# HGRN2 level scores in pairs of levels and 32-column tiles, diagonal from score blocks, block copies on GpSimd

## The chip, the core and the metric

The kernel runs on one core of a Trainium2 chip. The metric is the device time of one execution in microseconds; the time before is the median of three runs. The five engines are called TensorE (PE, its weight loads PEld), VectorE (DVE), ScalarE (ACT), GpSimd (POOL) and SyncE (SP, which here only issues DMAs).

## What is computed

One inference step of a one-layer encoder with two parallel branches, mLSTM and HGRN2, for a prompt of 512 frames and a running stream of 32 frames. Both are projected by one large input matrix; the branches' outputs are merged by sigmoid gates, projected, and normalised. The part that matters here is the HGRN2 scan over 8 heads of 128 channels. In chunk form it is

```python
def _hgrn_chunk(S, inp):
    q, k, v, lf = inp
    causal = jnp.tril(jnp.ones((L, L), dtype=bool))[:, :, None]
    g = jnp.cumsum(lf, axis=2)
    dec = jnp.exp(jnp.where(causal, g[:, :, :, None, :] - g[:, :, None, :, :], -jnp.inf))
    a = jnp.einsum('bhtc,bhtsc,bhsc->bhts', q, dec, k)
    o = jnp.einsum('bhtc,bhce->bhte', q * jnp.exp(g), S) + jnp.einsum('bhts,bhse->bhte', a, v)
    ...
```

The score of query t and key s is a sum over channels c of q, k and a decay that depends on t, s and c. So it is no plain matrix product.

## The kernel before, in words

All sequences lie side by side in 544 columns: 32 of the stream (NS) and 512 of the prompt (NP). Activations have channels on the 128 partitions and time on the columns. The large products are done in split precision (three fp32r products for one fp32 product), and pairs of output tiles share a Strassen-like scheme of seven block products, the class `Two`; its `run` (L608) issues 12 matmuls of 128 stationary and 272 moving columns per block and gives way after the sixth. A `Pump` works through a list of such blocks; `pump.to(n)` advances it by half-blocks of six matmuls. TensorE's order is thus written by hand (manual_schedule), while the order on VectorE, ScalarE, GpSimd and the DMA queues is chosen by a scheduler that takes instructions under `high_priority` first.

**The HGRN stage** is `chain(h)` for each of the 8 heads. It is a generator: each `yield n` lets the pump run n half-blocks of the projections that the following heads need, then the chain's own matmuls are issued. Per head there are 28 half-blocks.

**Levels.** Time is halved recursively. At level c (1, 2, 4 to 64) a query in the odd block of length c meets the keys in the even block before it. The kernel keeps keys `kk` and queries `qq` in one tile and multiplies both in place by the decay products of each level (L1850), so that at level c a plain product gives the scores of pairs that are c apart. Because the first half of the prompt is stored reversed, `view` picks the columns by strides. Per level:

- ScalarE copies the keys in level order into `km` (L1818), and for the four levels below 16 the stream's keys and queries into `snap` (L1823);
- TensorE issues two products of 128 x 128, fp32, into the PSUM tile `pl` (L1832); at level 16 also the stream's own (L1834) and one for the four snapshots together (L1836);
- VectorE multiplies keys and queries (L1850), makes the decay products of the next level (L1853, L1856), and copies the scores that belong to this level under a mask into `at` (L1857, and L1861 for the stream).

The diagonal (t = s) is made apart: VectorE multiplies q and k for all 544 columns into `kq` (L1725), TensorE transposes this in five pieces (L1871), and VectorE sums each row into `dg` (L1873). After the last level GpSimd keeps the triangle of each score block (`triangle`, L1797, output `aa`). Then values and keys are transposed (L1902; L1903 for the stream, whose 32 columns GpSimd repeats four times, L1888), the state update follows (`su`, L1921, L1922), the states are chained on VectorE (L1927), and the output products are issued (`ho`, L1945 to L1949). The head before is finished in `finish`.

What TensorE waits for in this loop: the `km` copy, which waits for the update L1850, which waits for the products of the level before, since these read `qq` itself. The PSUM tiles `pl`, `pd`, `ht`, `su`, `ho` all come from one ring of two.

**A place with column tiles.** The stream's value products at the start (L1586) write to 32 partitions each (`vq[j * NS : (j + 1) * NS]`), so their stationary operand has 32 columns, and four such products stand on different column groups of the array. The dense value products around them are at L1576.

Of the kernel before, what the change touches and what calls it, by code (L numbers as in the profile page):

```python
# [17 lines left out]
P = 128  # L18
# [18 lines left out]
QUADS = P // NS  # L37
STEPS = (2, 3, 3, 3, 3, 3, 3)
# [29 lines left out]
def hybrid_step(ctx: ExitStack, tc: tile.TileContext, a, o):  # L68
# [247 lines left out]
    def masks():  # L316

        t = cp.tile([P, T], F32, tag="lm", name="lmask")
        u, n = t[:, :T].bitcast(U8), len(LEVELS) * HB
        return u[:, :n].rearrange("p (l t) -> p l t", l=len(LEVELS)), u[:, n : n + NS]  # L320
# [1060 lines left out]
    def level_masks():  # L1381
        lmask, smask = masks()
        sxt = small("sxt", [P, P + 2 * NS], bufs=1, tag="vsm")
        nc.sync.dma_start(sxt, a["sxt"])
        for i, c in enumerate(LEVELS):
            V.tensor_scalar(
                lmask[:, i, : 2 * P].rearrange("p (b t) -> p b t", b=2),
                sxt[:, :P].rearrange("p (o t) -> p o t", o=1).to_broadcast([P, 2, P]),
                float(c),
                None,  # L1390
                ALU.is_ge,
            )
        V.tensor_scalar(smask, sxt[:, P : P + NS], 0.5, None, ALU.is_ge)
        V.tensor_scalar(lmask[:, QUADS, 2 * P :], sxt[:, P + NS :], 0.5, None, ALU.is_ge)
        return lmask, smask
# [227 lines left out]
    with tc.manual_schedule(engines={mybir.EngineType.PE}):  # L1623
        for h in range(MH):
# [46 lines left out]
            if h == 0:  # L1671
                with tc.issue_after(last.ins):
                    next(bounds)
                    lmask, smask = level_masks()
# [21 lines left out]
    def units():  # L1696
# [19 lines left out]
        def query(h, qq):  # L1716
# [8 lines left out]
            V.tensor_tensor(kq[:, :T], q0[:, :T], kk[:, :T], ALU.mult)  # L1725
# [75 lines left out]
    def chain(h):  # L1801

        tf, kk, q0, qq, kq, ii = (hs[h][k] for k in ("tf", "kk", "q0", "qq", "kq", "ii"))
        at = tp.tile([P, NA + P], F32, tag="bc", name=f"at{h}")
        G.memset(at, 0.0)
        snap = small("snap", [P, 2, QUADS, NS], bufs=1, tag="ksm")
# [4 lines left out]
        tsmp = None  # L1811
        for li, c in enumerate(LEVELS):
            smp = li == QUADS
            n = HB if smp else NA
            km = tp.tile([P, NA], F32, tag="vs", name=f"km{h}{c}", bufs=1)
            pump.behind = held[-1] if held else None
            with tc.high_priority():
                low = S.copy(  # L1818
                    km.rearrange("p (n j c) -> p n j c", j=2, c=c),
                    view(kk, HB, ((2 * c, NA // (2 * c)), (c - HB, 2), (1, c))),  # L1820
                )
                if li < QUADS:
                    S.copy(snap[:, :, li], hs[h]["pair"][:, :, csmp])  # L1823
            held.append(low)
            yield STEPS[li]

            pn = paux(f"pl{h}{c}")
            for b in range(2):
                out, dims = pn[:, 0, b * P : (b + 1) * P], ((2 * c, P // (2 * c)), (HB + c, 2), (1, c))
                if c == 1:  # L1830
                    out, dims = out.rearrange("p (i s) -> p s i", s=2), (dims[1], dims[0])
                PE.matmul(out, km[:, b * P : (b + 1) * P], view(qq, b * P, dims), start=True, stop=True)  # L1832
            if smp:
                PE.matmul(pn[:, 0, NA:HB], kk[:, NA : NA + P], qq[:, csmp], start=True, stop=True)  # L1834
                ks, qs = (snap[:, i].rearrange("p l t -> p (l t)") for i in range(2))
                PE.matmul(pn[:, 1, :P], ks, qs, start=True, stop=True)  # L1836
# [4 lines left out]
            with tc.high_priority():  # L1841
# [15 lines left out]
                V.copy_predicated(at[:, :n], lmask[:, li, :n], pn[:, 0, :n])  # L1857
                if smp:
                    for i in range(QUADS):
                        d = slice(i * NS, (i + 1) * NS)  # L1860
                        V.copy_predicated(at[d, NA:HB], smask[d], pn[d, 1, d])  # L1861
# [4 lines left out]
            if li == 0:  # L1866

                yield 1
                pn = paux(f"pd{h}")
                for b, c_ in enumerate([c_ for c_, _, _ in chunks] + [slice(NA, NA + P)]):  # L1870
                    PE.transpose(pn[:, b // NB, b % NB * P : (b % NB + 1) * P], kq[:, c_], ident)  # L1871
                with tc.high_priority():
                    V.tensor_reduce(  # L1873
                        dg, pn.rearrange("p a t -> p (a t)")[:, : 5 * P].rearrange("p (b t) -> p b t", t=P), AX.X, ALU.add
                    )
# [11 lines left out]
        def quads(src, i):  # L1887
            G.tensor_copy(snap[:, i], src[:, csmp].rearrange("p (o t) -> p o t", o=1).to_broadcast([P, QUADS, NS]))  # L1888
            return snap[:, i].rearrange("p l t -> p (l t)")

        kt, it = kk[:, :NP], ii[:, :NP]
        ov = kq
        osb = small("osb", [P, P])
        kit = small("kit", [P, 2, P], tag="qw")
        kts, its = kit[:, 0], kit[:, 1]
        s0 = small("s0", [P, P], tag="qf")
        nc.sync.dma_start(s0, a["S0"][h])
        for n, src, dst, dss in ((0, ii, it, its), (2, kk, kt, kts)):
            yield n
            pt = paux(f"ht{h}")  # L1900
            for b, (c, _, _) in enumerate(chunks):
# [393 lines left out]
```

## Time and profile before

| | us |
|---|---|
| median of 3 runs (lowest, highest) | 1103.63 (1103.42, 1103.95) |
| profiled execution, first to last instruction | 1101.5 |
| HGRN stage in it | about 627 to 873 |

The page gives the profiled execution's span, and no other time of it. In the rows that follow, a group is named by line, engine, operation and tiles (output<-inputs); "PE L1832 MATMUL ... x4" in a timeline is four passes, since an fp32 product runs as two passes, each with its own weight load. The times of a matmul's end are modelled, so the starts, above all those of the weight loads, say more about how TensorE proceeds than the lengths.

### The profile page before, as it was taken

The page shows a single profiled execution, that of the slowest core. Times are in us where ns is not written, and L with a number is a line of the kernel's source. Part 1 is how long each engine was busy: PE and PEld are TensorE (multiplying, and loading weights), DVE is VectorE, ACT ScalarE, POOL GpSimd, SP SyncE. Part 2 cuts the span into 40 slices and gives each one's busy share as a digit, 9 for nine tenths or more (in the row PEclk, how much of TensorE's full clock was granted, in tenths as well). Part 3 has the DMA queues.
Part 4 walks back from the last instruction along what each step waited for, and adds up shares of the span by engine and source line. Part 5 has one row for each costly group of instructions (what it writes and reads, how often), then busy time and mean ns, then how long its engine had stood idle before and what let it go on. Part 6 is the DMA issues. An engine that isn't in the chain of part 4 may idle for free.

```text
span 1101.5 us, 23773 instructions
## 1 busy us (share of the span) xinstructions
PE 1092.4 (99%) x8625; PEld 1070.9 (97%) x8625; DVE 922.8 (84%) x2103; ACT 693.1 (63%) x1579; POOL 209.5 (19%) x375
## 2 busy tenths in 40 slices
PE   9999999999999999999999999999999999999997
PEld 9899999999999999999999999999999999999997
DVE  7889988686896786986888799999999977778885
ACT  7777557754666554665656476776776666446683
POOL 5204010303022021202120123232232210000002
PEclk9999999999999999999999999999999999999999
DMA  7135415639355276554798665666765683337753
GB/s 241 50 124 157 156 58 185 158 125 220 119 178 179 93 178 176 164 167 146 212 261 254 172 145 141 144 135 152 159 145 150 155 222 103 110 90 242 247 180 121
DMA packets 97262, 176.58 MB, mean 160 GB/s; under 512 B 11284, under 2 KB 18580, under 8 KB 96888
## 3 DMA queue, kind: packets, MB, share of 16 engines
q1 hardware_dynamic: 81072, 141.01, 39.9%
q0 software_dynamic: 15184, 32.93, 16.2%
q8 instruction: 68, 1.11, 0.4%
q10 hardware_dynamic: 888, 1.12, 0.3%
q14 instruction: 50, 0.41, 0.1%
HBM read 150.10 MB, written 41.69 MB: 174 GB/s over the span
## 4 chain that ended last, share of the span: by engine, by line
PE 93%; DMA 3%; DVE 2%; issue 1%; SPq 0%; ACT 0%; POOL 0%; ACTq 0%; POOLq 0%
PE d L608 44%; PE ya L167 9%; PE yb L167 4%; PE q L167 4%; PE k L167 4%; PE C L1077 4%; PE nm L1257 3%; PE sc L1037 2%; PE pl L1832 2%; PE u L291 2%; PE d L460 2%; PE vp L1576 2%; DMA ws<-in_w_in 1%; PE ple L167 1%; PE kt L1122 1%; PE ht L1902 1%
## 5 line engine op out<-in xcount | busy, mean ns | idle before, releaser
L495 POOL DMA_DIRECT2D ws<-in_w_in x46 | 40.2, 875 | 211.3 <-DVE hkq L1850 32.2
L622 ACT COPY t<-d 128x272 f32<-128x272 f32 x153 | 58.0, 379 | 14.0 <-PE d L608 14.0
L1850 DVE TENSOR_TENSOR hkq<-hkq,q 128x288 f32<-128x288 f32 (+1 forms) x96 | 40.7, 431 | 2.6 <-PE pl L1834 1.0
L785 DVE SCALAR_TENSOR_TENSOR cv<-ub,vec,cv 128x547 f32<-128x547 f32 x48 | 37.6, 784 | 1.6 <-ACT cv L780 1.2
L1832 PE MATMUL pl<-hkq,km 128*128 128x128 f32 x224 | 36.2, 283 | 0.6 <-ACT km L1818 0.5
L1818 ACT COPY km<-hkq 128x256 f32<-128x256 f32 x56 | 23.9, 428 | 14.2 <-DVE hkq L1850 5.2
L1832 PEld LDWEIGHTS pl<-hkq,km 128*128 128x128 f32 x224 | 30.3, 189 | 2.0 <-ACT km L1818 1.5
L1191 DVE SCALAR_TENSOR_TENSOR c<-c,wi,Cs 128x258 f32<-128x258 f32 x32 | 15.3, 479 | 18.8 <-PE Cs L1189 18.5
L1354 DVE TENSOR_TENSOR y<-ya,y 128x272 f32<-128x272 f32 x48 | 18.9, 435 | 12.1 <-PE ya L167 10.3
L1089 ACT COPY Co<-C 128x258 f32<-128x258 f32 x30 | 9.8, 378 | 27.3 <-PE C L1077 24.9
L1857 DVE COPY_PREDICATED at<-lmask,pl 128x256 f32<-128x256 uint8 (+1 forms) x56 | 25.2, 451 | 0.1
L777 POOL COPY uo<-ub 128x3 f32<-128x3 f32 x16 | 18.7, 1167 | 34.5 <-DVE ub L631 26.6
L1268 ACT COPY y<-nm 128x516 f32<-128x516 f32 x16 | 9.4, 590 | 23.0 <-PE nm L1257 22.5
L133 POOL TENSOR_TENSOR wple50l<-wple5r,wple50h 128x256 fp32r<-128x256 f32 x1 | 0.7, 736 | 120.9 <-ACT wple50h L132 120.9
L961 POOL COPY ksm<-kf 128x96 f32<-128x96 f32 x16 | 7.1, 445 | 84.9 <-ACT kf L975 84.9
L961 POOL COPY vsm<-vt 128x96 f32<-128x96 f32 x12 | 6.3, 525 | 85.9 <-ACT vt L633 43.5
L1797 POOL TENSOR_SCALAR_AFFINE_SELECT aa<-at 128x128 f32<-128x128 f32 x32 | 19.6, 643 | 8.2 <-DVE at L1857 8.0
L581 POOL DMA_DIRECT2D ws<-in_w_in x14 | 14.6, 1043 | 33.1 <-DVE ws272l L133 27.3
L1245 DVE BATCH_NORM_STATS2 bs<-y 128x6 f32<-128x512 f32 (+1 forms) x20 | 13.8, 692 | 8.3 <-ACT y L1268 8.0
L1257 PE MATMUL nm<-vhl,sh 128*128 128x258 f32 x112 | 18.4, 286 | 0.0
L376 POOL DMA_DIRECT2D w_pg_d<-in_w_pg x16 | 13.1, 818 | 25.1 <-issue 21.4
L1956 ACT ACTIVATE osq<-kq 128x128 f32<-128x128 f32 x32 | 9.8, 305 | 12.4 <-DVE kq L1951 12.1
(4735 smaller groups left out, 5086.7 us busy)
## 6 DMA issues: line engine op xcount, KB each, us to landing
ws<-in_w_in POOLq DMA_DIRECT2D x60, 256.0 KB, 4.9
ws<-in_w_in SPq DMA_DIRECT2D x46, 256.0 KB, 3.9
ya_d<-y SPq DMA_DIRECT2D x32, 272.0 KB, 2.3
y<-ya_d SPq DMA_DIRECT2D x24, 272.0 KB, 3.3
w_out_d<-in_w_out POOLq DMA_DIRECT2D x24, 256.0 KB, 6.5
w_pg_d<-in_w_pg POOLq DMA_DIRECT2D x24, 256.0 KB, 6.5
c<-in_C SPq DMA_DIRECT2D x16, 258.0 KB, 3.8
out_Cs<-c SPq DMA_DIRECT2D x16, 258.0 KB, 3.8
```

The source lines that it names most:

```text
L167: PE.matmul(both[b][:m, :TH], part(w, off + k * step, m, x), xx[:, half(b)], start=(k == 0 and j == 0), stop=(k == n - 1 and j == 2),)
L291: PE.matmul(both[b][:m, :TH], part(w, off + k * step, m, x), xx[:, half(b)], start=(k == 0 and j == 0), stop=(k == KD - 1 and j == 2),)
L495: G.dma_start(t, piece(u, i), accum_op=ALU.add)
L608: PE.matmul(ps, ww[:, c], xx, start=(start and k == 0 and j == 0), stop=end, skip_group_check=not start,)
L622: self.kept = S.copy(t, ps)
L785: V.scalar_tensor_tensor(cv[:, :547], ub[:, j : j + 547], vcol(V_CW + 4 * ft + j), cv[:, :547], ALU.mult, ALU.add)
L1077: PE.matmul(pn[g][:, :VH], kw[b][x][:, f * P : (f + 1) * P], vv[b][y][:, g * VH : (g + 1) * VH], start=(b == 0 and j == 0), stop=(b == NB ...
L1257: PE.matmul(pn[:, g, :VH], st[j][x][:, (i - j) * P : (i - j + 1) * P], vv[j][y][:, g * VH : (g + 1) * VH], start=(j == 0 and q == 0), stop ...
L1818: low = S.copy(km.rearrange("p (n j c) -> p n j c", j=2, c=c), view(kk, HB, ((2 * c, NA // (2 * c)), (c - HB, 2), (1, c))),)
L1832: PE.matmul(out, km[:, b * P : (b + 1) * P], view(qq, b * P, dims), start=True, stop=True)
L1850: V.tensor_tensor(x, x, d, ALU.mult)
L1857: V.copy_predicated(at[:, :n], lmask[:, li, :n], pn[:, 0, :n])
```

## The change

1. **Column tiles.** `scores` issues a level's products as pieces: for each of the two score blocks and each group of 32 keys one product with 32 stationary columns and max(c, 32) query columns, written to the 32 partitions of that group. The stream's keys and queries get such a product at each level below 32, once per group.
2. **Pairs of levels.** Level 1 is done with the diagonal, then 2 with 4, 8 with 16, 32 with 64. For the first of a pair the queries are copied too (`oldq`, and `olds` for the stream, in what is left of the mask tile), so that keys and queries can be multiplied on before TensorE reads them. The chain gives way once per pair, for the sum of both levels' steps.
3. **Diagonal.** Twenty products of 32 x 32 beside level 1 hold q times k; VectorE multiplies by an identity (`eye`) and sums five rows of 32. The product L1725 and the transposes L1871 go.
4. **Collecting.** Levels below 32 go under a mask into `near` (96 columns, five masks in place of seven). Level 32 is copied whole into `far` and level 64 straight into the off-diagonal halves of `at`, by ScalarE. At the end GpSimd copies the 32 x 32 blocks from `near` and `far` into `at`, and then makes the triangles as before. These copies are outside `high_priority`.
5. **Value transposes early.** `columns(ii, ...)`, the products with `dg` and the load of the state `s0` follow level 1; the keys' transposes stay behind the last level. The stream's columns are no longer repeated by GpSimd; a cleared tile `kit` takes the 32 rows.

```diff
+        def scores(pn, i, c, km, snap):
+            for b in range(2):
+                for g in range(QUADS):
+                    key, w = b * P + g * NS, max(c, NS)
+                    out = pn[g * NS : (g + 1) * NS, i, b * w : (b + 1) * w]
...
+                    PE.matmul(out, km[:, key : key + NS], ask, start=True, stop=True)
+            if c < NS:
+                for g in range(QUADS):
+                    PE.matmul(
+                        pn[g * NS : (g + 1) * NS, i, 2 * NS : 3 * NS],
+                        olds[:, 0] if snap else kk[:, csmp],
+                        olds[:, 1] if snap else qq[:, csmp],
...
+        def collect(ps, li, c):
+            if c < NS:
+                V.copy_predicated(near, lmask[:, li], ps[:, : 3 * NS])
+            elif c == NS:
+                S.copy(far, ps[:, : 2 * NS])
+            else:
+                for g in range(2):
+                    k = slice(g * c, (g + 1) * c)
+                    S.copy(
+                        at[k, :NA].rearrange("p (b s t) -> p b s t", b=2, s=2)[:, :, 1 - g],
...
         for li, c in enumerate(LEVELS):
-            km = tp.tile([P, NA], F32, tag="vs", name=f"km{h}{c}", bufs=1)
+            first_ = li % 2 == 1
+            if li % 2 == 1 or li == 0:
+                kms = tp.tile([P, 2, NA], F32, tag="vs", name=f"km{h}{c}", bufs=1)
+            km = kms[:, 0 if li % 2 else 1]
             with tc.high_priority():
+                if first_:
+                    S.copy(oldq..., view(qq, ...))
+                    if c < NS:
+                        S.copy(olds, hs[h]["pair"][:, :, csmp])
                 low = S.copy(km..., view(kk, ...))
-                if li < QUADS:
-                    S.copy(snap[:, :, li], hs[h]["pair"][:, :, csmp])
-            held.append(low)
-            yield STEPS[li]
+            if not first_:
+                held.append(low)
+                yield STEPS[li] + (STEPS[li - 1] if li else 0)
+                pn = paux(f"pl{h}{c}")
+                if li:
+                    scores(pn, 0, c // 2, kms[:, 0], True)
+                else:
...
+                            PE.matmul(
+                                pn[g * NS : (g + 1) * NS, 0, b * NS : (b + 1) * NS], kk[:, t_], q0[:, t_], start=True, stop=True
+                            )
+                scores(pn, 1, c, km, False)
...
-                V.copy_predicated(at[:, :n], lmask[:, li, :n], pn[:, 0, :n])
+            if not first_:
+                if li == 0:
+                    V.tensor_tensor(same, pn[:, 0, : (NB + 1) * NS].rearrange("p (b t) -> p b t", t=NS), eye, ALU.mult)
+                    V.tensor_reduce(dg, same, AX.X, ALU.add)
+                else:
+                    collect(pn[:, 0], li - 1, c // 2)
+                collect(pn[:, 1], li, c)
+            if c == 2 * NS:
+                for g in range(QUADS):
...
+                    G.tensor_copy(at[k, :NA].rearrange("p (b q s t) -> p b q s t", b=2, q=2, s=2)[:, :, g // 2], both_)
             if li == 0:
                 yield 1
-                    PE.transpose(pn[:, b // NB, b % NB * P : (b % NB + 1) * P], kq[:, c_], ident)
+                columns(ii, it, its)
```

How the instructions stand now, at three places. The names are the program's tiles with their numbers: `pl28` is the score tile of head 2 at level 8, `hkq2` holds its keys and queries, `lmask` the masks and the copied queries; rows of the changed kernel carry its own line numbers. On TensorE, head 2 before, from level 1 to level 16 (dense products left out):

```order
L1832 MATMUL pl21_9982<-hkq2_9364,km21_9959 128x2x64 x2
...
L1871 MATMUL pd2_10001<-ident_104,kq2_9365 128x128 x5
...
L1832 MATMUL pl22_10037<-hkq2_9364,km22_10008 128x128 x2
...
L1832 MATMUL pl24_10082<-hkq2_9364,km24_10044 128x128 x2
...
L1832 MATMUL pl28_10129<-hkq2_9364,km28_10089 128x128 x2
...
L1832 MATMUL pl216_10168<-hkq2_9364,km216_10136 128x128 x2
L1834 MATMUL pl216_10168<-hkq2_9364 128x32
L1836 MATMUL pl216_10168<-snap_9957 128x128
```

And now, to the last level:

```order
L1894 MATMUL pl21_10118<-q02_9852,hkq2_9430 32x32 x20
L1841 MATMUL pl21_10118<-hkq2_9430,km21_10096 32x2x16 x8
L1844 MATMUL pl21_10118<-hkq2_9430 32x32 x4
...
L1818 MATMUL ht2_10170<-ident_104,hi2_9703 128x128 x4
...
L1841 MATMUL pl24_10253<-lmask_2764,km22_10184 32x32 x8
L1844 MATMUL pl24_10253<-lmask_2764 32x32 x4
L1841 MATMUL pl24_10253<-hkq2_9430,km22_10184 32x32 x8
L1844 MATMUL pl24_10253<-hkq2_9430 32x32 x4
...
L1841 MATMUL pl264_10478<-lmask_2764,km232_10410 32x32 x8
L1841 MATMUL pl264_10478<-hkq2_9430,km232_10410 32x64 x8
```

Two products of 128 x 128 per level have become 8 to 12 of 32 columns, a visit holds two levels, and the values' transposes stand ahead of level 2. On ScalarE, head 2 before, levels 4 to 16:

```order
L1818 COPY km24_10044<-hkq2_9364 128x256
L1823 COPY snap_9957<-hkq2_9364 128x2x32
L132 CAST ws175h_10106<-ws175_9863 128x512
L622 COPY t16751_10065<-d510_9836 128x272
L1711 ACTIVATE hkq3_9838<-kq3_9839 128x256
L622 COPY t175_10098<-d750_10072 128x272
L1818 COPY km28_10089<-hkq2_9364 128x256
```

And now, levels 8 and 16:

```order
L1873 COPY lmask_2764<-hkq2_9430 128x256
L1878 COPY lmask_2764<-hkq2_9430 128x64
L1879 COPY km28_10283<-hkq2_9430 128x256
L1705 ACTIVATE tf3_10341<-kq3_9974 128x256
L634 ACTIVATE kq3_9974<-d510_9971 128x272
L1879 COPY km28_10283<-hkq2_9430 128x256
```

The first of a pair has three copies in a row (queries, stream, keys), and the second's copy of the keys follows after two instructions of the next head. On GpSimd, the end of head 2's scores before, and then now:

```order
L581 DMA ws175_9863<-in_w_in 128x512
L1888 COPY snap_9957<-hi2_9601 128x128
L495 DMA ws376_10340<-in_w_in 128x512
L1888 COPY snap_9957<-hkq2_9364 128x128
L1797 AFFINE_SELECT aa2_10283<-at2_9955 128x128 x4
L495 DMA ws153_10574<-in_w_in 128x512
```

```order
L582 DMA ws175_9997<-in_w_in 128x512
L496 DMA ws376_10543<-in_w_in 128x512
L1935 COPY at2_10089<-at2_10089 32x2x64 x4
L1790 AFFINE_SELECT aa2_10505<-at2_10089 128x128 x4
L582 DMA ws152_10299<-in_w_in 128x512
L496 DMA ws153_10842<-in_w_in 128x512
```

The four block copies stand directly ahead of the four triangles, and the weight DMAs of the next head stand behind both.

More of the change, by code (lines that the diff above doesn't have):

```diff
@@ L37 @@
 QUADS = P // NS
+SUB = 5
 STEPS = (2, 3, 3, 3, 3, 3, 3)
@@ L1803, in chain @@
         tf, kk, q0, qq, kq, ii = (hs[h][k] for k in ("tf", "kk", "q0", "qq", "kq", "ii"))
[L1804 to L1806 removed]
+        at = tp.tile([P, NA + 6 * NS], F32, tag="bc", name=f"at{h}")
+        near, far = at[:, NA : NA + 3 * NS], at[:, NA + 3 * NS : NA + 5 * NS]
+        G.memset(at[:, NA:], 0.0)
         dg = small("dg", [P, 5])
@@ L1811, in chain, with columns @@
         tsmp = None
+        kit = small("kit", [P, 2, P], tag="qw")
+        G.memset(kit, 0.0)
+        oldq, olds = old[:, :NA], old[:, NA : NA + 2 * NS].rearrange("p (l t) -> p l t", l=2)
+        eye = old[:, NA + 2 * NS :].rearrange("p (o t) -> p o t", o=1).to_broadcast([P, NB + 1, NS])
+        kt, it, ov = kk[:, :NP], ii[:, :NP], kq
+        kts, its = kit[:, 0], kit[:, 1]
+        osb = small("osb", [P, P])
+        s0 = small("s0", [P, P], tag="qf")
+        def columns(src, dst, dss):
+            pt = paux(f"ht{h}")
+            for b, (c, _, _) in enumerate(chunks):
+                PE.transpose(pt[:, 0, b * P : (b + 1) * P], src[:, c], ident)
+            PE.transpose(pt[:, 1, :P], src[:, NA : NA + P], ident)
+            with tc.high_priority():
+                S.copy(dst, pt[:, 0, :])
+                S.copy(dss[:NS], pt[:NS, 1, :P])
@@ L1868, in chain @@
                 yield 1
[L1869 to L1875, printed above, removed]
+                columns(ii, it, its)
+                nc.sync.dma_start(s0, a["S0"][h])
+                for b in range(NB):
+                    S.mul(ov[:, b * P : (b + 1) * P], it[:, b * P : (b + 1) * P], dg[:, b : b + 1])
+                S.mul(osb, its, dg[:, 4:5])
             if li == (4 if h < HH - 1 else 6) and h:
@@ L1884, in chain @@
                 triangle(aa[:, j, b], at[:, b * P : (b + 1) * P], 1 - 2 * j)
[L1887 to L1901, printed above, removed]
-                PE.transpose(pt[:, 0, b * P : (b + 1) * P], src[:, c], ident)
-            PE.transpose(pt[:, 1, :P], quads(src, n // 2), ident)
-            with tc.high_priority():
-                S.copy(dst, pt[:, 0, :])
-                if n:
-                    S.mul(dss, pt[:, 1, :P], 1.0 / QUADS)
-                else:
-                    S.copy(dss, pt[:, 1, :P])
-            if n == 0:
-                for b in range(NB):
-                    S.mul(ov[:, b * P : (b + 1) * P], it[:, b * P : (b + 1) * P], dg[:, b : b + 1])
-                S.mul(osb, its, dg[:, 4:5])
+        yield 2
+        columns(kk, kt, kts)
         yield 2
```

83 lines of the change are left out of this document (44 added, 39 removed).

## The prediction

> **What bounds the kernel now.** I read the page first: span, busy engines, and the chain that ended last.
>
> ```profile
> span 1101.5 us, 23773 instructions
> PE 1092.4 (99%) x8625; PEld 1070.9 (97%) x8625; DVE 922.8 (84%) x2103; ACT 693.1 (63%) x1579; POOL 209.5 (19%) x375
> PE 93%; DMA 3%; DVE 2%; issue 1%; SPq 0%; ACT 0%; POOL 0%; ACTq 0%; POOLq 0%
> ```
>
> TensorE is busy from end to end and holds 93% of the last chain. "Busy" alone proves little, because matmuls are pipelined, so I asked for the waits of TensorE over the whole span, and for the busy times of the HGRN stage, which is the only stage that the change touches.
>
> ```profile
> PE pl L1832 <- ACT km L1818: 0.5, 1, 0.5
> 627.00:873.00 246.00, 245.33 (x1993) 242.66 (x1992) 237.44 (x651) 175.00 (x485) 69.31 (x100) 1.00 0.64 148
> ```
>
> The first row is the only wait of TensorE inside the stage: 0.5 us in 246 us. In the second row the columns after the length are PE, PEld, DVE, ACT and POOL. TensorE issues without a break, so its time here is the sum of its passes. VectorE is at 237.4 of 246 us, but what it delivers is on time. A head takes about 30.7 us (246 us for eight heads), and a microsecond of TensorE time saved per head is worth 8 us at the end, as long as nothing starts to wait.
>
> **The change, TensorE's part.** What goes is read from the starts of the weight loads, which follow each other without gaps.
>
> ```profile
> 701.09 0.54 PEld L1832 LDWEIGHTS pl<-hkq,km 128*128 128x128 f32 x4
> 701.55 0.30 PEld L1834 LDWEIGHTS pl<-hkq 128*128 128x128 f32 x2
> 701.77 0.30 PEld L1836 LDWEIGHTS pl<-snap 128*128 128x128 f32 x2
> 701.99 0.19 PEld L608 LDWEIGHTS d<-xh,ws451h 128*128 128x128 f32 x1
> 690.05 0.58 PEld L1871 LDWEIGHTS pd<-ident,kq 128*128 128x128 f32 x5
> 690.60 0.19 PEld L608 LDWEIGHTS d<-xfh,ws251h 128*128 128x128 f32 x1
> ```
>
> An fp32 product is two passes. The two products of a level (x4) take 701.55 - 701.09 = 0.46 us, 115 ns a pass; the two sample products at level 16 take 0.22 us each; the five diagonal transposes 690.60 - 690.05 = 0.55 us. Per head: 7 x 0.46 + 0.44 + 0.55 = 4.21 us, over eight heads 33.7 us.
>
> What comes: per head 96 products with 32 stationary columns, 32 in the first visit (20 for the diagonal, 12 for level 1), then 24, 24 and 16. That is 192 passes in place of 37. They go to four column tiles in turn, 48 passes a tile; in 44 of these 32 columns move, in 4 (level 64) 64. Nothing in this stage works like that, but the start of the program has such a place. The timeline of the value products (L1576) around the sample value products (L1586, 32 stationary columns, four tiles):
>
> ```profile
> 46.79 0.40 PE L1576 MATMUL vp<-wv3h,x 128*128 128x512 f32 x1
> 47.03 0.40 PE L1576 MATMUL vp<-wv3l,x 128*128 128x512 f32 x1
> 47.36 0.62 PE L1586 MATMUL vq<-wv0r,xg 128*32 128x512 f32 x1
> 47.36 0.62 PE L1586 MATMUL vq<-wv1r,xg 128*32 128x512 f32 x1
> 47.81 0.59 PE L1586 MATMUL vq<-wv0r,xg 128*32 128x512 f32 x1
> 47.83 0.59 PE L1586 MATMUL vq<-wv3r,xg 128*32 128x512 f32 x1
> 48.35 0.72 PE L1576 MATMUL vp<-wv4h,x 128*128 128x512 f32 x2
> 48.91 0.40 PE L1576 MATMUL vp<-wv4l,x 128*128 128x512 f32 x1
> 47.35 0.11 PEld L1586 LDWEIGHTS vq<-wv0r,xg 128*32 128x32 f32 x1 [0.37 <-issue]
> 47.38 0.11 PEld L1586 LDWEIGHTS vq<-wv0r,xg 128*32 128x32 f32 x1
> ```
>
> Three things are to be seen. Different tiles run side by side: wv0r and wv1r both start at 47.36. One tile's second pass starts 47.81 - 47.36 = 0.45 us after its first, 0.88 ns a column, and its second load starts 0.03 us after its first load, while the first pass runs. And going in and out costs: dense passes stand 0.24 us apart, so the last ended at 47.27 and the tiles began at 47.36, 0.09 us; the last tile pass ended at 47.83 + 0.45 = 48.28, and the third dense pass at 48.91 puts the first at about 48.44, 0.16 us. I price a visit at 0.25 us, four visits at 1.0 us a head.
>
> The passes themselves: at 0.88 ns a column and with loads fully hidden, 44 x 28 + 4 x 56 ns = 1.46 us a head. With a tile's load (30 ns) and pass (28 ns) one after the other it is 44 x 58 + 4 x 86 = 2.9 us. I take 40 ns for the short pass and 70 for the long one, 2.04 us, nearer to the hidden end, since the rows show a load under a running pass. Then a head pays 1.0 + 2.04 = 3.04 us (2.46 to 3.9) for the 4.21 us removed: 1.17 us less, over eight heads 9.4 us (14 to 2.5).
>
> The value transposes (five passes) are only moved from behind the last level to behind the first; no pass is added, and the dense products between stay 28 half-blocks a head.
>
> **The other engines.** The groups of one head, 690 to 720 us, by form:
>
> ```profile
> L1857 DVE COPY_PREDICATED at<-lmask,pl 128x256 f32<-128x256 uint8 x6 | 2.7, 445 | 0.0
> L1861 DVE COPY_PREDICATED at<-lmask,pl 32x32 f32<-32x32 uint8 x4 | 0.8, 190 | 0.0
> L1873 DVE TENSOR_REDUCE dg<-pd 128x5 f32<-128x640 f32 x1 | 0.8, 819 | 0.0
> L1725 DVE TENSOR_TENSOR kq<-q,hkq 128x544 f32<-128x544 f32 x1 | 0.7, 720 | 0.0
> L1818 ACT COPY km<-hkq 128x256 f32<-128x256 f32 x7 | 3.0, 427 | 1.8 <-DVE hkq L1850 1.0 <-DVE hr L185 0.5 <-DVE rsq_u L184 0.4
> L1823 ACT COPY snap<-hkq 128x64 f32<-128x64 f32 x4 | 1.0, 247 | 0.0
> L1888 POOL COPY snap<-hi 128x128 f32<-128x128 f32 x1 | 0.6, 596 | 0.0
> L1888 POOL COPY snap<-hkq 128x128 f32<-128x128 f32 x1 | 0.3, 293 | 1.2 <-DVE hkq L1850 1.2
> 711.16 2.59 POOL L1797 TENSOR_SCALAR_AFFINE_SELECT aa<-at 128x128 f32<-128x128 f32 x4 [1.18 <-DVE at L1857]
> ```
>
> VectorE loses about 5 us of these (the level-16 mask copy with them) and gains five masked copies of 96 columns, about 0.26 us each on the line between 190 ns at 32 and 445 at 256 columns, and two operations over 160 columns, about 0.3 us each: some 3 us less in 30.7. That buys no time by itself, since TensorE did not wait for VectorE, but it loosens the tightest helper. ScalarE loses four snapshots (1.0 us) and gains three copies of the queries (427 ns each), two of the samples (247 each) and three block copies out of PSUM (about 250 each): about 1.5 us more, in an engine at 175 of 246 us. Neither counts on TensorE's path, except in the hand-over below. GpSimd loses the two broadcast copies and half a memset and gains a memset and four copies of 32 partitions; the mask tables are made once and under dense products.
>
> **The hand-over.** What is new is the wait. Before, TensorE did one level per visit, with 18 dense products until the next; now two levels in 36. The row of steps of one level before:
>
> ```profile
> 698.84 0.38 PE L608 MATMUL d<-xfh,wa2251h 128*128 128x272 f32 x1
> 699.21 0.46 DVE L1850 TENSOR_TENSOR hkq<-hkq,q 128x288 f32<-128x288 f32 x1
> 699.91 0.42 DVE L1850 TENSOR_TENSOR hkq<-hkq,q 128x256 f32<-128x256 f32 x1
> 700.44 0.41 ACT L1818 COPY km<-hkq 128x256 f32<-128x256 f32 x1 [0.48 <-DVE hr L185]
> ```
>
> From the resumption of dense work (698.84) to the end of the copy (700.85) is 2.0 us; the next level's load came at 701.09, so 18 products gave 2.25 us and 0.24 us were to spare. Now two such hops with three copies for the one (0.43 + 0.25 more), about 4.7 us, stand against 36 products, 4.5 us, plus the visit's own first half, 0.3 us or so, because only its second half needs the later copy. That is just enough. I put 0.2 us of waiting per head into the sum, 1.6 us.
>
> Sum: -9.4 + 1.6 = -7.8 us. The profiled span of 1101.5 becomes 1093.7; the runs of before have a median of 1103.6, 2.1 us above the span, which is outside the first and last instruction and stays: 1095.8 us.
>
> **The rivals.**
>
> *Passes do not overlap (chance 0.12).* The four tiles of the rows above had passes of 512 columns, sixteen times longer than these; no row shows short ones. If short passes start one by one at the 30 ns of a load whatever their tile, 192 take 5.8 us, with the visits 6.8, and a head is 2.6 us longer: 21 us, 1124 us. Against it stands that loads of different tiles began within 10 ns. The Trainium skill (TensorE: Matmul & The Clock Gate, section "Wait — 56ns, not 53.3ns?") puts the start-to-start of matmuls at no less than about 25 ns however few columns move; an estimate by that page is 192 x 25 ns = 4.8 us, 1116 us. The rows at 47.36 speak against it, as far as they go.
>
> *The hand-over decides (chance 0.15, slower).* The wait that the copies make takes the place of the time saved. If on each of the two VectorE hops one more 0.7 us instruction stands ahead, half of it covered, visits two to four wait 0.7 us each: 24 x 0.7 = 17 us, against 9.4 saved: 1111 us. It decides from 0.39 us a visit. For it: the slack was 0.24 us, and VectorE issues in order. Against: VectorE has 3 us less to do per head, and masked copies no longer stand ahead of the updates.
>
> *It does not do what it says (chance 0.09).* Loads and passes of a tile serialize and something is lost at each start; the price comes to the 4.2 us removed: 1103.6, within 0.2%.
>
> *GpSimd is late (chance 0.07).* After the last level come ScalarE's copies (about 1.5 us), four GpSimd copies (0.3 to 0.6 us each by the rows of L1888), and the four triangles, 2.6 us: 5.3 to 6.5 us. TensorE reaches the output products after 36 dense products (4.5 us), five transposes (0.55) and ten state passes at 0.11 us (1.1): 6.15 us. It loses at most 0.35 us a head, 3 us: 1098.6, still faster.
>
> **How the numbers follow.** My forecast has 0.57. Its own range is 1088 (cheapest passes, no wait, a little from the loosened VectorE) to 1103 (dearest passes). A measurement of this kernel tells 0.2%, 2.2 us, from no change. Faster by more than that: 0.53 of the forecast and the late GpSimd, 0.60. Within: 0.04 of the forecast and the third rival, 0.13. Slower: 0.15 + 0.12 = 0.27. The range takes in the hand-over and leaves the first rival out: 1088 to 1111 us.
>
> **What would show it.** In the profile after, the weight loads of a visit of 64 passes should span about 0.6 to 0.9 us until the dense products go on, the next ones less; four tiles should start within some 30 ns of each other. If loads stand 25 ns or more apart throughout, the first rival holds. Waits of TensorE for the query or key copies should stay under 2 us in all; 10 or more is the second. VectorE should fall by about 25 us in the stage. The forecast is wrong if the stage is not shorter, or if the saving appears in the stage and is lost behind it.

## The result, and the profile after

The changed kernel takes 1091.93 us (median of 4 runs, 1091.56 to 1093.22) where the kernel before takes 1103.72 (1103.42 to 1103.95): a ratio of 0.9892, 95% interval 0.9879 to 0.9904, 11.8 us less. The forecast was 1095.8, 7.9 us less; the range of 1088 to 1111 holds the time. The profiled execution is the longest of the four.

The page after, span, engines and the chain that ended last:

```profile
span 1091.5 us, 26220 instructions
PE 1082.2 (99%) x9865; PEld 1055.3 (97%) x9865; DVE 896.1 (82%) x2052; ACT 700.6 (64%) x1611; POOL 220.1 (20%) x399
PE 89%; DVE 4%; DMA 4%; issue 1%; ACT 1%; POOL 0%; ACTq 0%; DVEq 0%; SPq 0%; POOLq 0%
```

TensorE still bounds the kernel. The HGRN stage, from its first score product to its last output product, in the busy times by stretch (before, then after; columns as in the prediction):

```profile
627.75:870.62 242.87, 242.20 (x1968) 239.53 (x1966) 235.21 (x646) 173.52 (x479) 67.84 (x99) 1.00 0.64 147
```

```profile
628.06:861.46 233.40, 231.40 (x3206) 223.80 (x3206) 211.45 (x607) 181.18 (x512) 78.14 (x121) 1.00 0.66 154
```

The stage is 9.5 us shorter in these two executions. VectorE has 23.8 us less to do in it, ScalarE 7.7 more, GpSimd 10.3 more. The waits of TensorE in the stage after:

```profile
PE ht L1818 <- DVE hkq L1911: 1.4, 2, 0.8
PE d L609 <- DVE ws288l L134: 0.6, 1, 0.6
```

No wait for a copy of queries or keys is among them. The profiled execution is the slowest of its four; in that of c_after below (the changed kernel once more) the first row is 0.3 us in place of 1.4.

**A visit.** The timeline of TensorE around the second visit of head 2 (48 passes), dense products ahead and behind:

```profile
693.59 0.29 PE L609 MATMUL d<-xh,wa1175l 128*128 128x272 f32 x1
693.81 0.33 PE L1841 MATMUL pl<-lmask,km 128*32 128x32 f32 x16
693.96 0.25 PE L1844 MATMUL pl<-lmask 128*32 128x32 f32 x8
694.02 0.32 PE L1841 MATMUL pl<-hkq,km 128*32 128x32 f32 x14
...
694.37 0.39 PE L609 MATMUL d<-xh,wa1175h 128*128 128x272 f32 x1
694.60 0.29 PE L609 MATMUL d<-xl,wa1175h 128*128 128x272 f32 x1
```

The start of the first product behind a visit can't be taken as it stands (the next comes 0.23 us after it, where dense ones stand about 0.125 apart), so I measure from the last dense product ahead (693.59) to the second behind (694.60): 1.01 us, less two dense slots, 0.76 us for the visit. In the same way one level of head 2 before:

```profile
698.31 0.29 PE L608 MATMUL d<-xh,wa1275l 128*128 128x272 f32 x1
698.44 0.66 PE L1832 MATMUL pl<-hkq,km 128*128 128x128 f32 x4
698.84 0.38 PE L608 MATMUL d<-xfh,wa2251h 128*128 128x272 f32 x1
699.06 0.29 PE L608 MATMUL d<-xfl,wa2251h 128*128 128x272 f32 x1
```

That is 0.75 - 0.25 = 0.50 us. Measured like this over all heads (from the third dense product ahead to the fourth behind, less six slots of 0.1237 us), the medians are: before, a level 0.489, level 16 with the stream 0.907, the five diagonal transposes 0.559, level 64 0.571 (it stands with the values' transposes: 1.127 for both, less 0.556 for these); after, the visits 0.916 (64 passes), 0.772 (48, twice) and 0.697 (32). Sixteen passes more or less are 0.144 us, 9 ns a pass, 36 ns a pass of one tile; what is left of each visit, 0.34 us, is the price of going in and out. The rows show the same: the 16 passes of the first kind start at 693.81, the next kind at 693.96. The slot is a little short: the dense products of the stage stand 0.126 us apart in the median, and with that every stretch is some 0.012 us shorter. The price per pass does not move by it; the price of going in and out becomes 0.33 us, and what is summed over the heads below differs by 0.3 us between before and after.

**The hand-over.** Between the second and the third visit of head 2, copies of the keys (L1879) and the third visit's loads; the rows between them left out:

```profile
698.32 0.42 DVE L1911 TENSOR_TENSOR hkq<-hkq,q 128x256 f32<-128x256 f32 x1
...
698.77 0.41 ACT L1879 COPY km<-hkq 128x256 f32<-128x256 f32 x1
...
699.11 0.22 PEld L1841 LDWEIGHTS pl<-lmask,km 128*32 128x32 f32 x16
...
699.29 0.25 PEld L1841 LDWEIGHTS pl<-hkq,km 128*32 128x32 f32 x15
```

The second copy ends at 699.18, while the visit's first half runs, 0.11 us ahead of the load that reads it. The other two hops have about 1 us more, since the values' transposes or the finish of the head before, with a half-block each, lie in them; the finish is missing from this place in the first and the last head, and there the third hop is as tight as the second. GpSimd at the end of a head, by groups of the page:

```profile
L1935 POOL COPY at<-at 32x128 f32<-32x128 f32 x32 | 21.7, 678 | 8.4 <-DVE wa1282l L134 6.7
L1790 POOL TENSOR_SCALAR_AFFINE_SELECT aa<-at 128x128 f32<-128x128 f32 x32 | 16.1, 536 | 0.6
```

Block copies and triangles take 4.7 us a head, and no wait of TensorE for them is among the rows. The mean of the block copies hides a spread: 0.28 us at the least, 0.51 in the median, and four of the 32 take 2.0 to 2.1 us, for a reason that stays open.

### The profile page after: what moved, and what is told of

Same layout as the page of the kernel before. It is cut to its first block, busy times and chain, and to the rows that moved or that the text cites. A ratio compares the mean times of both kernels' runs of the same rounds, so it can differ in the third digit from the quotient of the medians.

```text
span 1091.5 us, 26220 instructions
## 1 busy us (share of the span) xinstructions
PE 1082.2 (99%) x9865; PEld 1055.3 (97%) x9865; DVE 896.1 (82%) x2052; ACT 700.6 (64%) x1611; POOL 220.1 (20%) x399
## 4 chain that ended last, share of the span: by engine, by line
PE 89%; DVE 4%; DMA 4%; issue 1%; ACT 1%; POOL 0%; ACTq 0%; DVEq 0%; SPq 0%; POOLq 0%
PE d L609 41%; PE ya L168 9%; PE yb L168 4%; PE q L168 4%; PE k L168 4%; PE C L1078 4%; PE sc L1038 2%; PE u L292 2%; PE d L461 2%; PE vp L1570 2%; PE nm L1258 2%; DMA ws<-in_w_in 2%; PE ple L168 1%; PE pl L1841 1%; DMA kv_d<-vhl 1%
## 5 line engine op out<-in xcount | busy, mean ns | idle before, releaser
L1879 ACT COPY km<-hkq 128x256 f32<-128x256 f32 x56 | 23.7, 424 | 0.0
L1935 POOL COPY at<-at 32x128 f32<-32x128 f32 x32 | 21.7, 678 | 8.4 <-DVE wa1282l L134 6.7
L2001 ACT ACTIVATE osq<-kq 128x128 f32<-128x128 f32 x32 | 9.8, 305 | 13.4 <-DVE kq L1996 13.1
L377 POOL DMA_DIRECT2D w_pg_d<-in_w_pg x16 | 13.1, 818 | 24.4 <-issue 20.2
L377 POOL DMA_DIRECT2D w_out_d<-in_w_out x16 | 13.5, 1004 | 14.3 <-issue 12.5
L1790 POOL TENSOR_SCALAR_AFFINE_SELECT aa<-at 128x128 f32<-128x128 f32 x32 | 16.1, 536 | 0.6
L1258 PEld LDWEIGHTS nm<-vhl,sh 128*128 128x128 f32 x112 | 15.4, 190 | 0.5 <-ACT Co L1090 0.3
```

Of the source, the lines that this page charges most:

```text
L377: G.dma_start(late[g][n][k], src, accum_op=ALU.add)
L1258: PE.matmul(pn[:, g, :VH], st[j][x][:, (i - j) * P : (i - j + 1) * P], vv[j][y][:, g * VH : (g + 1) * VH], start=(j == 0 and q == 0), stop ...
L1879: low = S.copy(km.rearrange("p (n j c) -> p n j c", j=2, c=c), view(kk, HB, ((2 * c, NA // (2 * c)), (c - HB, 2), (1, c))),)
```

## The experiments

My theory after the result: TensorE's own sum decides (passes of 9 ns, 0.34 us to enter and leave), and the waits stay where they were because every hop fits, the tightest by 0.1 us. The rivals: the narrow passes alone are the gain; or VectorE's relief is; or one of the smaller moves (values, block copies, urgency) is.

The last column is the time that all the chain's own matmuls take on TensorE in the stage, measured as above around each stretch of them and summed over the eight heads. Waits are in it, their own and those of the dense products right beside them. In the first pair it is 77.3 us before and 66.7 after.

| kernel | median us | before, timed beside it | ratio (95%) | chain on TensorE, us |
|---|---|---|---|---|
| c_after, the change again | 1092.08 | 1104.48 | 0.9887 (0.9872, 0.9902) | 65.4 |
| e1_tiles_single | 1100.24 | 1104.72 | 0.9960 (0.9946, 0.9974) | 73.6 |
| e2_stream_once | 1094.69 | 1104.72 | 0.9911 (0.9896, 0.9925) | 67.3 |
| e3_diag_old | 1102.16 | 1104.72 | 0.9973 (0.9961, 0.9986) | 76.9 |
| e4_short | 1099.70 | 1104.72 | 0.9957 (0.9942, 0.9972) | 75.1 |
| e5_shift | 1105.08 | 1104.48 | 1.0006 (0.9997, 1.0015) | 77.4 |
| e6_copies_act | 1095.92 | 1104.48 | 0.9924 (0.9911, 0.9938) | 69.8 |
| e7_values_late | 1098.94 | 1104.48 | 0.9952 (0.9936, 0.9969) | 71.4 |
| e8_urgent | 1097.22 | 1104.23 | 0.9946 (0.9929, 0.9963) | 69.9 |
| e9_load | 1093.96 | 1104.23 | 0.9904 (0.9889, 0.9918) | 67.3 |
| e10_shift_add | 1093.44 | 1104.23 | 0.9903 (0.9888, 0.9918) | 67.2 |
| e11_add | 1092.66 | 1104.23 | 0.9896 (0.9881, 0.9911) | 66.4 |

A thousandth of the ratio is 1.1 us. Against c_after's ratio, the kernels' last column and their time rise together: what these edits do, they do on this chain. "Over the change" below means by the difference of the two ratios. Only e5 to e7 were timed beside c_after; with the ratio of the first pair, 0.9892, each of these figures is 0.6 us smaller.

**c_after.** 

> The changed kernel itself, unaltered, timed beside the next three on their chip. Expected 10 to 12 us under the kernel before, as in its first runs.

It came out so, 12.4 us under the kernel before.

**e1_tiles_single: tiles without pairs.**

```diff
-            first_ = li % 2 == 1
+            first_ = False
...
-                yield STEPS[li] + (STEPS[li - 1] if li else 0)
+                yield STEPS[li]
...
-                if li:
-                    scores(pn, 0, c // 2, kms[:, 0], True)
```

> The changed kernel with its column tiles and its diagonal, but one level per visit: seven visits a head instead of four, no copies of the queries. Theory (entering and leaving a visit is what costs: 0.34 us, and a pass 9 ns, by the gaps in the dense products around the visits of 64, 48 and 32 passes): three more visits are 3 x 0.34 x 8 = 8 us more than the changed kernel, so about 1100 us, only 3 to 4 us under the kernel before. Rival (the narrow passes are the gain, and the pairing only a convenience): within 2 us of the changed kernel, 1090 to 1094. Second rival (the pairing costs waits that single levels do not have): under 1091.

It is 8.1 us over the change, and 4.5 under the kernel before: the theory's number. The visits of 24 passes cost 0.536 us (median of 32), which again is 0.32 + 24 x 9 ns. So a level with the stream in narrow passes, 0.54, costs more than the 0.49 of its four wide passes. Alone, the tiles pay at level 16, where the stream's wide products go (0.907 before), and at level 1, where the diagonal rides along; the rest comes when two levels share one way in and out. The rival of narrow passes alone is refuted. Pairs in wide passes were not run; as four wide passes, which start 0.119 us apart, pay only 0.01 us beyond their own time (0.489 less four of 0.119), an estimate from these prices is that three visits fewer would save 3 x 0.01 x 8 = 0.2 us.

**e2_stream_once: fewer passes, unevenly.**

```diff
             if c < NS:
-                for g in range(QUADS):
+                for g in range(1):
...
-                V.copy_predicated(near, lmask[:, li], ps[:, : 3 * NS])
+                V.copy_predicated(near[:, : 2 * NS], lmask[:, li, : 2 * NS], ps[:, : 2 * NS])
+                V.copy_predicated(near[:NS, 2 * NS :], lmask[:NS, li, 2 * NS :], ps[:NS, 2 * NS : 3 * NS])
```

> The changed kernel with the stream's product of each level below 32 issued for the first group of 32 partitions only (the other three are multiplied by zero later), and its masked copy as a piece of its own of 32 partitions (five more short VectorE instructions a head). 30 of 192 passes a head go, all from three of the four column tiles; the first tile keeps its 48. If a visit lasts as long as the queue of passes (8 to 9 ns each, whatever the tile): 30 x 0.0085 x 8 = 2 us less than the changed kernel, about 1090. If it lasts as long as the fullest tile (32 to 36 ns a pass of one tile): no change, 1091 to 1093. If the five VectorE instructions delay the hand-over: above 1094.

The visits did get shorter, 0.855 and 0.702 us for 0.916 and 0.772: six passes gone take 0.06 us off the first visit and twelve 0.07 off the next two, 10 and 6 ns each, nearer to the queue's case than to the fullest tile's. The time did not: 2.6 us over the change, where the two intervals still overlap. What is lost is not the hand-over, as I had expected of the third case, but at the dense products, which wait for the splits of their weights:

```profile
PE d L609 <- DVE ws288l L134: 1.3, 1, 1.3
PE d L609 <- DVE ws276l L134: 0.3, 1, 0.3
...
PE d L609 <- DVE ws279l L134: 0.3, 1, 0.3
```

With the new instructions the scheduler's order on VectorE is another: ahead of the split of `ws274` stand a masked copy and an operation on a dense result that stand behind it in c_after. In six heads the stretch beside it, the transposes of `finish`, takes 1.16 us instead of 0.56.

**e3_diag_old: the diagonal of before.** The product L1725, the transposes and the sum come back, and the twenty products of 32 x 32 go (short form):

```diff
+            V.tensor_tensor(kq[:, :T], q0[:, :T], kk[:, :T], ALU.mult)
...
-                    V.tensor_tensor(same, pn[:, 0, : (NB + 1) * NS].rearrange("p (b t) -> p b t", t=NS), eye, ALU.mult)
-                    V.tensor_reduce(dg, same, AX.X, ALU.add)
...
+                pn = paux(f"pd{h}")
+                for b, c_ in enumerate([c_ for c_, _, _ in chunks] + [slice(NA, NA + P)]):
+                    PE.transpose(pn[:, b // NB, b % NB * P : (b % NB + 1) * P], kq[:, c_], ident)
...
                 columns(ii, it, its)
```

> The changed kernel with the diagonal of before: the product of queries and keys over 544 columns on VectorE, five transposes of 128 x 128 on TensorE, one sum over 640 columns; the first visit has 24 passes instead of 64. TensorE by the prices: five transposes 0.56 us for 40 passes of 9 ns, 0.2 us a head more, so 1.6 us in all, about 1093.5. Rival (the 0.9 us a head that VectorE gets back are what loosens the hand-over): waits of TensorE come back with it, 1096 or more.

9.5 us over the change: the rival, not the sum. The waits of TensorE, and the third visit of head 2 in the timeline:

```profile
PE pl L1842 <- ACT km L1880: 2.4, 6, 0.5
PE ht L1819 <- DVE hkq L1905: 2.3, 4, 0.9
```

```profile
699.62 0.42 DVE L1905 TENSOR_TENSOR hkq<-hkq,q 128x256 f32<-128x256 f32 x1
...
699.92 0.33 PE L1842 MATMUL pl<-lmask,km 128*32 128x32 f32 x16
...
700.26 0.40 ACT L1880 COPY km<-hkq 128x256 f32<-128x256 f32 x1
...
700.72 0.33 PE L1842 MATMUL pl<-hkq,km 128*32 128x32 f32 x16 [0.40 <-ACT km L1880]
```

Here the update stands 0.3 us ahead of the visit (after: 698.32 against 699.11, 0.8 us), so the visit breaks in two. The hand-over is the change's weak place, and the new diagonal is part of what holds it. Measured by stretches and summed over the heads, the third visits take 3.5 us more than their median after the change, the keys' transposes, which wait for the last update, 5.9 (4.2 of it in two heads), the state's products 2.0, and the passes themselves 1.3. This execution is the slowest of ten that lie between 1099.4 and 1104.5 us, so the shares are rough.

**e4_short: a shorter hand-over.**

```diff
-                yield STEPS[li] + (STEPS[li - 1] if li else 0)
+                yield STEPS[li] + (STEPS[li - 1] - 1 if li else 0)
```

> The changed kernel with five half-blocks ahead of each pair instead of six (30 dense products instead of 36; the rest run later). It asks how much slack the hand-over has. If it is just enough, as the record has it and as the copy that ends 0.1 us ahead of its use shows: visits two to four each wait about 0.6 us, 24 x 0.6 = 14 us, 1104 to 1108. If VectorE and ScalarE get the steps earlier because what was ahead of them in their queues is later too: half of that or less, 1092 to 1098.

7.7 us over the change, between the two cases: visits two to four are 0.74 us earlier each, 17.8 us in all, and less than half of that comes back as waits.

```profile
PE pl L1841 <- ACT km L1879: 6.5, 10, 1.1
PE ho L1990 <- POOL aa L1790: 2.0, 2, 1.5
```

So the hop from the second visit to the third gives way at once, those with 1 us to spare mostly do not. The second row is new: where TensorE arrives earlier, it meets GpSimd's triangles.

**e5_shift and e10_shift_add: one half-block elsewhere.**

```diff
-                yield STEPS[li] + (STEPS[li - 1] if li else 0)
+                yield STEPS[li] + (STEPS[li - 1] - (li == 2) if li else 0)
...
-        yield 2
+        yield 3
         columns(kk, kt, kts)
```

> The changed kernel with one half-block (six dense products) moved within each head: five instead of six ahead of the second visit, where the copy of the keys ends 1.0 us before it is read, and three instead of two ahead of the transposes of the keys, where TensorE waits 1.4 us in all. If that wait is the only loss there: 1 to 1.5 us less than the changed kernel. If the second visit gets late instead (0.74 us of its 1.0 us of slack are used): no change or up to 3 us more. If the hop from the second visit to the third, whose slack is 0.1 us, shifts with it: 2 to 6 us more.

None of my cases: 13.1 us over the change, no faster than the kernel before, though the third visits are longer by only 0.05 us in most heads. The waits of TensorE, and the timeline of head 2 in front of the keys' transposes:

```profile
PE ht L1818 <- DVE hkq L1911: 10.2, 6, 2.9
```

```profile
702.90 0.87 POOL L582 DMA_DIRECT2D ws<-in_w_in  x1 [0.34 <-DVE ws275l L134]
```

```profile
708.32 0.62 ACT L133 CAST ws475h<-ws 128x512 fp32r<-128x512 f32 x1 [1.42 <-DMA ws<-in_w_in]
...
709.23 0.38 PE L1818 MATMUL ht<-ident,hkq 128*128 128x128 f32 x2
709.92 0.39 ACT L623 COPY t<-d 128x272 f32<-128x272 f32 x1
710.34 0.17 DVE L632 SCALAR_TENSOR_TENSOR hi<-d,t 128x16 f32<-128x16 f32 x1 [1.64 <-ACT t L623]
710.43 0.42 DVE L1911 TENSOR_TENSOR hkq<-hkq,q 128x256 f32<-128x256 f32 x1
```

Read backwards: the transposes wait for the keys' last update (710.43). That stands in VectorE's queue behind an operation that waits for ScalarE's copy of a dense result (709.92). The copy stands behind the cast of `ws475`, with the next copies between them, and the cast waits for a transfer that adds the last weights onto a sum. GpSimd issues it when VectorE has split the sum before, at 702.90; it lands at 708.24, and the cast starts 5.4 us after the issue. In the changed kernel the same two steps are these, ahead of the fourth visit, where in e5 the cast comes behind it:

```profile
701.37 0.87 POOL L582 DMA_DIRECT2D ws<-in_w_in  x1 [2.02 <-DVE hkq L630]
```

```profile
705.59 0.62 ACT L133 CAST ws475h<-ws 128x512 fp32r<-128x512 f32 x1
```

By this reading no engine is short of time: the queues of GpSimd, ScalarE and VectorE keep their order and pass one late transfer on to TensorE. To test that, e10 makes the same sum on VectorE:

```diff
-            if self.early and form == "s2" and not self.alone:
-                G.dma_start(q["s4"], piece(a, 1), accum_op=ALU.add)
-            elif form == "s2" if self.grows else form in ("s2", "a12") and "s2" in self.w and "a12" in self.w:
+            if form == "s2" if self.grows else form in ("s2", "a12") and "s2" in self.w and "a12" in self.w:
```

> The kernel with one half-block moved from ahead of the second visit to ahead of the keys' transposes (which lost 13 us), and in it the last weight sum of each pair of blocks added by VectorE (0.69 us) from a tile that is there, in place of an accumulating transfer that GpSimd issues. If the 13 us came from that transfer (the cast of its weights waits for it on ScalarE, the copies behind the cast wait too, then VectorE's update of the keys, then the transposes): the wait at the transposes falls from 10 us to under 2, and the time to 1092 to 1097. If the update was late for VectorE's own load: the wait stays or grows, 1104 or more.

The wait is gone and the time is 1.8 us over the change, as the first case had it. The same place in it:

```profile
704.74 0.62 ACT L133 CAST ws475h<-ws 128x512 fp32r<-128x512 f32 x1
...
706.87 0.42 DVE L1909 TENSOR_TENSOR hkq<-hkq,q 128x256 f32<-128x256 f32 x1
...
707.17 0.60 PE L1816 MATMUL ht<-ident,hkq 128*128 128x128 f32 x4
```

**e11_add: that sum on VectorE, nothing shifted.** Only the second of the two edits.

> The changed kernel with that sum on VectorE and no half-block moved. If the transfer's landing is what the rest of its waits at the keys' transposes hang on (0.3 to 1.4 us in the profiles): up to 1.5 us less than the changed kernel, 1090.5 to 1092. If VectorE's 0.69 us a head more make the hop from the second to the third visit late: 3 to 8 us more.

1.0 us over the change, the intervals overlap: neither case. The transfer costs the changed kernel little as long as it lands in time, and VectorE carries 0.69 us a head more: in six heads the fourth visit with the dense products beside it takes 0.93 to 1.13 us instead of 0.70. It is no better version; none of these is.

**e6_copies_act and e7_values_late: block copies, value transposes.**

```diff
-                    G.tensor_copy(at[k, :NA].rearrange("p (b q s t) -> p b q s t", b=2, q=2, s=2)[:, :, g // 2], both_)
+                    S.copy(at[k, :NA].rearrange("p (b q s t) -> p b q s t", b=2, q=2, s=2)[:, :, g // 2], both_)
```

> The changed kernel with the block copies at the end of a head on ScalarE in place of GpSimd (four of 32 partitions, about 0.25 us each there; on GpSimd the four took 3.4 us in the stretch behind 707.6 us of the trace). If GpSimd's chain of copies and triangles is hidden behind the dense products, as it seems (no wait of TensorE for the triangles in the changed kernel): no change, within 1.5 us. If it ends just too late in some heads: 1 to 3 us less. If the copies stand ahead of the state's or the keys' copies in ScalarE's queue: 2 to 6 us more.

4.1 us over the change, the third case: the four copies take 0.30 us each on ScalarE (0.68 in the mean on GpSimd), but they stand ahead of the copy of the transposed keys, and the state products wait for that.

```profile
PE su L1966 <- ACT hkq L1821: 3.1, 7, 0.8
```

In e7 the block `columns(ii, it, its)` to `S.mul(osb, ...)` is moved from level 1 to behind the triangles.

> The changed kernel with the value transposes, their copies, the products with the diagonal and the state's load back behind the last level. TensorE has the same passes, so if only sums count: no change, within 1.5 us. If the move is what keeps the hand-over: the work on ScalarE (five products with the diagonal and two copies, 2.4 us a head) leaves the first hop and comes into the stretch where the block copies, the keys' copies and the state are made, and the five passes no longer lengthen the first hop: waits at the keys' transposes or the state, 3 to 8 us more.

7.2 us over the change, within the second case, at the places that it named:

```profile
PE ht L1818 <- ACT kit L1822: 2.6, 4, 1.1
PE su L1967 <- ACT hkq L1821: 1.2, 5, 0.4
```

**e8_urgent: collecting under high priority.**

```diff
                 else:
-                    collect(pn[:, 0], li - 1, c // 2)
-                collect(pn[:, 1], li, c)
+                    with tc.high_priority():
+                        collect(pn[:, 0], li - 1, c // 2)
+                with tc.high_priority():
+                    collect(pn[:, 1], li, c)
```

> The changed kernel with the collecting of the scores (five masked copies on VectorE, three copies out of PSUM on ScalarE a head) urgent, as the masked copies were before. If it matters that they are not urgent: each masked copy of 0.26 us comes ahead of an update on the way to the next copy of the keys, and the hop from the second to the third visit, with 0.1 us of slack, loses 0.2 to 0.4 us a head: 2 to 4 us more than the changed kernel. If the scheduler puts them where they are now anyhow: within 1.5 us of it.

6.5 us over the change, so urgency matters, but not where I had put it: the visits are as before the edit (0.770 us, median of 16), and TensorE's dense products wait for the splits of their weights, which now stand behind the masked copies.

```profile
PE d L609 <- DVE ws288l L134: 1.5, 1, 1.5
PE d L609 <- DVE ws275l L134: 0.5, 1, 0.5
```

Five more rows of 0.5 us follow these.

**e9_load: only VectorE's time.** The first added line of e3 alone, its product unused.

> The changed kernel with the product of queries and keys over 544 columns made again on VectorE (0.72 us a head) and not used; its result is overwritten. It asks whether the 9 us that the old diagonal cost more came from VectorE's time. If from VectorE's time as such: 5 to 8 us more than the changed kernel, about 1098 to 1100. If from the old diagonal's place (its sum over 640 columns ahead of the updates of the second hop, and the transposes): within 2 us, 1091 to 1094.

1.9 us over the change, inside "within 2 us", and the intervals overlap. What it costs is at one place: in six heads the fourth visit with the dense products beside it takes 0.96 to 0.98 us instead of 0.70, as a weight load behind it waits for VectorE's split (0.22 to 0.24 us). So most of the 9.5 us of e3 is not VectorE's time as such; it comes with the old diagonal's place, its sum and its transposes between the first visits. Which of these it is was not separated.

## Why the prediction was right, point by point

**What bounds the kernel: right, but for small waits.** TensorE's passes set the stage; 11.8 us less is what they and their waits lost. The record took 0.5 us for the only wait of the stage before, and VectorE for always in time. The table's measure has 2.9 us beyond the passes, and 1.4 of them stand behind the keys' transposes of six heads, 0.24 us each, where a weight load waits for VectorE's split:

```profile
711.91 0.19 PEld L608 LDWEIGHTS d<-xh,wa1252l 128*128 128x128 f32 x1 [0.19 <-DVE wa1252l L133]
```

The row that the record read is from the list of the matmuls' waits, which does not have these; the rows of the weight loads show them.

**What goes: too small.** The record had 4.21 us a head. Measured around the stretches it is 5 x 0.489 + 0.907 + 0.559 + 0.571 = 4.48 us. The starts of the weight loads gave a level 0.46 us from its first load to the next kind's first; the dense product that follows starts later than that. 0.27 x 8 = 2.2 us that the forecast missed.

**What comes: right to 4%, by two errors that cancel.** The record had 3.04 us; it is 0.916 + 2 x 0.772 + 0.697 = 3.16 us. A visit costs 0.34 us to enter and leave, not 0.25; a short pass of one tile 36 ns, not 40. The passes of one place at the start of the program, sixteen times wider, gave a good price per column (64 columns came close to its 56 ns); that the sum of both prices came out is luck.

**The other engines: right in size.** VectorE fell by 23.8 us in the stage (the record: about 25), ScalarE rose by 7.7 (1.5 a head, or 12). The sentence that this "buys no time by itself" does not hold. The six waits for a split, 1.4 us, are gone after the change, and e9 and e11, which give VectorE about 0.7 us a head back, get such waits again. The hand-over is another matter: the old diagonal breaks it (e3), the time alone does not (e9).

**The hand-over: right in mechanism, the wait did not come.** The record had 4.7 us against 4.5 plus 0.3 for the visit's first half, which leaves 0.1 us, and yet it put 0.2 us of waiting a head into the sum. From the first dense load behind the second visit of head 2 (694.37), the copies end after 4.8 us and the third visit reads them after 4.9; with 0.1 us to spare there is no wait in the rows. In most heads only this one of three hops is that tight, since the transposes of the values and the finish lengthen the others, which the record did not count. 1.6 us of the forecast's error.

**The sum.** -7.8 us, less 2.2 for what goes, plus 1.0 for what comes (0.12 x 8), less 1.6 for the wait: -10.6. The chain on TensorE shows -10.6 in the profiled pair. The other waits of the chain are what is left of its sums after the passes (before 77.3 - 74.4 = 2.9 us; after 2.8 in the profiled execution and 1.5 in c_after's), so they account for up to 1.4 us more, and the median is 11.8 us down. The forecast had two thirds of this.

**The rivals.** *Passes do not overlap:* refuted. Passes start 9 ns apart, and one tile's 32 to 36 ns apart; the weight loads of a visit of 64 passes span 0.71 us until the dense ones go on, as the forecast said they would (0.6 to 0.9). The floor of about 25 ns between starts that the Trainium skill states (TensorE: Matmul & The Clock Gate, section "Wait — 56ns, not 53.3ns?") does not hold across column tiles here; the measurement decides. *The hand-over decides:* it did not. With 0.74 us less at each hop (e4) 7.7 us come back, but the kernel stays 5 us faster than before. *It does not do what it says:* refuted, though e1, tiles without pairs, comes within 4.5 us of it. *GpSimd late:* its block copies took 0.68 us in the mean, 0.51 in the median (the record: 0.3 to 0.6), its triangles 0.54 in the mean for 0.65, and it is on time by little: e4 makes TensorE wait for it.

## What to carry to other kernels

A narrow column-tile pass costs little and the way in and out costs much, so count visits before passes: here two levels a visit were the whole difference between 4.5 and 12 us. Where engines keep their order, a move worth 0.7 us can cost 13 by putting one late transfer ahead of a chain, so read backwards through three queues before calling an engine short of time. Where a hop fits by 0.1 us and the weights' splits come just in time, a small edit mostly loses: of eleven variants here none was faster. A list of the matmuls' waits can miss what their weight loads wait for, so read both.

## What the runs showed of the hardware

- 32-column fp32 passes spread over four column tiles start 9 ns apart by the lengths of the visits (36 ns for one tile); by the starts alone a tile's next pass comes 32 ns after its last through the first half of a visit. When three of four tiles have fewer, the visit still shortens, by 6 to 10 ns for each pass gone. A pass of 64 columns in one tile costs about 53 ns (0.697 - 0.34 us less four passes of 36, over four); by the starts the next comes 55 to 60 ns later.
- Going from dense 128-column fp32r products into column tiles and back costs 0.32 to 0.34 us, as against 0.01 us for fp32 passes over all 128 columns (0.489 less four passes of 0.119, their median distance in the levels before).
- For a copy of 128 elements on 32 partitions ScalarE takes 0.30 us every time (0.29 to 0.30, e6); GpSimd takes 0.28 to 2.07 us, 0.51 in the median.
